# The left operands of a Strassen-type product: seven turned operands, or four turned blocks and sums of the turned blocks

## The chip, the cores and the metric

The kernel runs on 1 core of one Trainium2 chip. The metric is the time on the device in microseconds (us). The engines are TensorE (PE, matmuls; its weight loads are listed apart as PEld), VectorE (DVE), ScalarE (ACT), GpSimd (POOL) and SyncE (SP), which issues the DMAs of the part of the program that matters here.

## The reference

One encoder layer is computed for two requests with the same weights, x_prompt of 512 rows and x_sample of 1024 rows, all of width 1024, in fp32:

```python
h = _rmsnorm(x, norm_attn_g[l])
z = h @ w_in[l]
...
x = x + jnp.concatenate([a_out, c], axis=-1) @ w_out[l]
h = _rmsnorm(x, norm_ffn_g[l])
u = _dwconv(h @ w_up[l], ffn_dw_w[l], ffn_dw_b[l])
x = x + (jax.nn.silu(u[..., :D_FF]) * u[..., D_FF:]) @ w_down[l]
...
return _rmsnorm(x, norm_final_g)
```

a_out is windowed attention and c a convolution branch. D_FF is 2816. The change concerns `h @ w_up` of the sample: its left factor h, 1024 rows by 1024, is cut in four blocks of 512 by 512.

## The kernel before, in words

**The product.** The sample's up-projection is a product of the Strassen kind. For each of 22 column groups j there are seven block products of 512 x 512 (first to seventh in the code) in place of eight. Each is computed in a split precision: an operand is kept as hi and lo in fp32r, and each of four inner steps c takes three matmuls, whi by hi, whi by lo and wlo by hi (`prod`, L1080 to 1095; the matmuls are L1089 to 1091). The left operands are needed with the inner dimension on the partitions, so PE turns them: four transposes of 128 x 128 against an identity fill one PSUM bank (L1012), ACT copies the bank to hi (L1014) and DVE takes lo as bank minus hi (L965). A[i, c] holds the pair for operand i and step c. The operands 1 and 2 are the plain blocks of the sample's first 512 normalised rows, left and right half; the operands 3 to 7 are sums of blocks, or plain blocks of the last 512 rows.

**The stages.** The sample's rows come in eight blocks of 128, i = 4 to 11 in the code. `out_half` (L727) makes a row block of the output projection in matmuls L736 to 738, adds the residual (L741) and takes the sum of squares on ACT (L747); POOL makes the reciprocal root of it in two small operations (L186, L187); `scaled` (L978) multiplies the row block by it and by the norm's weights on DVE. For the last 512 rows `scaled` does this in two halves (L987) and then also takes the Strassen sums of the row blocks on DVE (s1, s2, the difference in place, and `last_sum`). `turned(1)` and `turned(2)` run in the out-projection stage, in banks called b. The other five, in the order 4, 6, 7, 5, 3, come after it in four banks called t: 80 transposes, put on PE between the matmuls of second(0), fourth(0) and second(1), seven, seven and eight groups of four (`every`, L1266 to 1276). Behind that come fourth(1), with two dummy matmuls (L1156) that open the accumulating bank for a copy from ACT (L1290), and sixth(0), sixth(1), seventh(0), seventh(1). A sixth product accumulates in a bank w; ACT copies the result out of the bank into a tile called u2 (L1172), and seventh accumulates in the same bank.

**What sets the order.** From `by_hand` (L1248) on PE's order is the order of the program; on the other engines, and on PE before, it is set by the scheduler when the program is built. Tiles in SBUF come from a list of slots (q, c, h, d and s, of fixed sizes and counts; h is the 128 x 512 one, 61 of them). A tile takes the slot that has been free the longest, and gives it back when the program drops its last name. An instruction that writes a reused slot waits until the readers of the tile that had it before are done. In the rows of the program below, h0_1252 is slot h0, tile number 1252. POOL takes the lo of the right operands (L965), from a hi that ACT makes (L1075).

Of the kernel before, what the change touches and what calls it, by code (L numbers as in the profile page):

```python
# [15 lines left out]
P = 128  # L16
# [132 lines left out]
def tile_hybrid_encoder(ctx: ExitStack, tc: tile.TileContext, xs, rel_bias, norm_attn_g, w_in,  # L149
# [811 lines left out]
    def add(out, a, b, eng=None):  # L961
        (eng or nc.vector).tensor_tensor(out, a, b, op=ALU.add)  # L962

    def sub(out, a, b, eng=None):
        (eng or nc.vector).tensor_tensor(out, a, b, op=ALU.subtract)  # L965
# [12 lines left out]
    def scaled(i):  # L978

        t, b = divmod(i - 4, 4)  # L980
        x = rows[t, b] = sb.tile([D])
        if t == 0:
            nc.vector.scalar_tensor_tensor(x[:], x1[i][:], rs2[:, i:i + 1], gFb[:], op0=ALU.mult, op1=ALU.mult)
            x1.pop(i)
            return
        for s in (R, L):
            nc.vector.scalar_tensor_tensor(x[:, s], x1[i][:, s], rs2[:, i:i + 1], gFb[:, s], op0=ALU.mult, op1=ALU.mult)  # L987
# [7 lines left out]
        if i >= NB - 2:  # L995
            last_sum(b)

    def last_sum(b):
        sub(rows[0, b][:, L], rows[0, b][:, R], rows["s2", b][:])

    def block_rows(i, b):
        if i in (1, 2, 3):
            return rows[0, b][:, R if i == 2 else L]
        if i in (4, 7):
            return rows[1, b][:, R if i == 4 else L]
        return rows["s1" if i == 5 else "s2", b][:]

    def turned(i, get):
        for c in range(4):
            held, ap = get()  # L1010
            for b in range(4):
                nc.tensor.transpose(ap[:, b * P:(b + 1) * P], block_rows(i, b)[:, c * P:(c + 1) * P], ident[:])  # L1012
            hi, lo = A[i, c] = (sb.tile([NT], F32R), sb.tile([NT], F32R))
            nc.scalar.copy(hi[:], ap)  # L1014
            sub(lo[:], ap, hi[:].bitcast(F32))
            held = None
            yield 0.0
        key = {6: "s2", 5: "s1", 7: 1, 3: 0}.get(i)
        for b in range(4):
            rows.pop((key, b), None)  # L1020

    def old_bank():
        b = bank("turn")
# [81 lines left out]
    for i in range(4, NB - 2):  # L1105
        if i + NE < NB:
            side.appendleft(conv_norm(i + NE))
        if i == 8:
            pace.update(rate=RE)
            side.appendleft(turned(1, old_bank))  # L1110
        for n in range(2):
            out_blocks(i, n)
    reserve(4)
# [1 line left out]
        for half in range(2):  # L1115
            load_up(j, half)
    drain(side)
    for b in range(2):
        last_sum(b)
# [6 lines left out]
    side.append(turned(2, old_bank))  # L1126
    sums_up(0)
    sums_up(1)
    out_blocks(NB - 2, 1)
# [35 lines left out]
    def second(j, between=None):  # L1165
        prod(st[j]["x"][:, L], j, 2, False, True, between)
# [7 lines left out]
    def fourth(j, between=None, start=False):  # L1174
        prod(st[j]["x"][:, R], j, 4, start, True, between)
# [79 lines left out]
    def chain(*gens):  # L1255
        for g in gens:
            yield from g
# [410 lines left out]
```

## Time and profile before

| | |
|---|---|
| median of three runs | 1549.37 us (1546.07 to 1552.7) |
| the profiled execution by itself | 1546.14 us |
| its span in the trace | 1544.4 us |
| mean granted clock of TensorE | 0.99 |
| TensorE busy | 1490.0 us, 96% of the span |
| ACT L1014, 128x512 hi from a t bank, in the stage | 590 ns |
| transposes L1012, into t / into b | 80 / 32 |

Times in the trace count from the start of the span. A row of the timeline gives the start, the duration, the engine, the line, the operation, output <- inputs by the program's names (slot numbers left out), the shape and how many like it run on; in brackets at its end stands how long its engine was idle before it, and what released it. A row of the waits gives the engine, the line and the releaser, then the total, the number of times and the longest. A row of the windows gives the stretch, its length, then busy us and number of instructions of PE, PEld, DVE, ACT and POOL, the granted clock, the share of time that the DMA engines were busy and GB/s.

### The profile page before, as it was taken

Reading aid. Unit: us, or ns where it says so; the run is one execution under the profiler, and the core shown is the slowest. Engines: PE = TensorE matmul, PEld = TensorE weight load, DVE = VectorE, ACT = ScalarE, POOL = GpSimd, SP = SyncE. Lnnn points to the kernel's source line nnn. Section 1 sums busy time; section 2 is a strip of 40 time slices with the busy share of each in tenths; the row PEclk is TensorE's granted clock in tenths of the full one; section 3 lists DMA queues with packets and bytes.
Section 4 is the critical chain, followed back from the end, with each engine's and each line's share of the span. In section 5 each row is a group of like instructions: output and inputs, shape, how many; then the busy total and the mean of one; then the engine's idle time right before and its main releaser. Section 6 shows DMA issues by size and latency. Waiting matters only on the chain. (4 is left out here: it accounts for less than half of the span.)

```text
span 1544.4 us, 20112 instructions
## 1 busy us (share of the span) xinstructions
PE 1490.0 (96%) x6843; PEld 1227.7 (79%) x6843; DVE 1126.2 (73%) x1604; ACT 795.5 (52%) x1404; POOL 710.7 (46%) x566
## 2 busy tenths in 40 slices
PE   8899998999999999899999999999999999999996
PEld 6787787787888888777777888888888788888885
DVE  6998767858789786344768777777776845569883
ACT  4644654335787786623454444545545543444354
POOL 7652343226666766957333555555554000003355
PEclk9999999899999999999999999999999999999998
DMA  6572334447344335769322233333331582357634
GB/s 229 160 214 79 108 98 129 130 135 226 112 130 134 117 124 182 245 234 300 129 80 87 86 102 108 112 106 105 103 116 67 194 291 83 106 167 235 220 136 164
DMA packets 228780, 227.17 MB, mean 147 GB/s; under 512 B 13268, under 2 KB 168348, under 8 KB 228549
## 3 DMA queue, kind: packets, MB, share of 16 engines
q1 hardware_dynamic: 228677, 225.88, 45.3%
q8 instruction: 54, 0.88, 0.2%
q14 instruction: 49, 0.40, 0.1%
HBM read 164.74 MB, written 62.14 MB: 147 GB/s over the span
## 5 line engine op out<-in xcount | busy, mean ns | idle before, releaser
L203 POOL TENSOR_TENSOR q<-q,q 128x1024 fp32r<-128x1024 f32 x72 | 173.5, 2415 | 91.5 <-ACT q L202 35.3
L965 POOL TENSOR_TENSOR q<-q,q 128x512 fp32r<-128x512 f32 x101 | 141.2, 1405 | 157.4 <-ACT q L1075 145.4
L965 DVE TENSOR_TENSOR h<-h,h 128x512 fp32r<-128x512 f32 (+2 forms) x202 | 153.8, 795 | 65.0 <-ACT h L969 24.4
L1423 PE MATMUL w<-h,h 128*128 128x512 f32 x462 | 179.8, 389 | 0.6 <-DVE q L1210 0.6
L1425 PE MATMUL w<-h,h 128*128 128x512 f32 x462 | 179.7, 389 | 0.0
L1424 PE MATMUL w<-h,h 128*128 128x512 f32 x462 | 179.7, 389 | 0.0
L1089 PE MATMUL w<-h,q 128*128 128x512 f32 x448 | 175.0, 391 | 2.9 <-ACT w L1181 1.2
L1091 PE MATMUL w<-h,q 128*128 128x512 f32 x448 | 174.4, 389 | 1.1 <-POOL q L965 1.1
L1090 PE MATMUL w<-h,q 128*128 128x512 f32 x426 | 165.8, 389 | 0.0
L309 PE MATMUL u<-h,q 128*128 128x512 f32 x400 | 159.4, 399 | 5.2 <-DVE h L862 4.3
L310 PE MATMUL u<-h,q 128*128 128x512 f32 x400 | 157.5, 394 | 0.0
L312 PE MATMUL u<-h,q 128*128 128x512 f32 x384 | 151.5, 394 | 2.8 <-POOL q L203 2.8
L962 POOL TENSOR_TENSOR q<-q,q 128x1024 f32<-128x1024 f32 x12 | 33.8, 2823 | 233.3 <-DMA h<-gb 194.4
L364 DVE SCALAR_TENSOR_TENSOR c<-c,cvw,c 128x512 f32<-128x512 f32 x184 | 138.0, 750 | 2.9
L969 ACT CAST h<-h 128x512 fp32r<-128x512 f32 x120 | 72.0, 620 | 93.2 <-DVE h L965 44.9
L309 PE MATMUL b<-h,q 128*128 128x512 f32 x256 | 102.3, 400 | 4.0 <-DVE d L394 3.0
L1423 PEld LDWEIGHTS w<-h,h 128*128 128x128 f32 x462 | 86.7, 188 | 19.1 <-ACT h L969 1.0
L862 DVE SCALAR_TENSOR_TENSOR h<-u,fw,h 128x511 f32<-128x511 f32 x88 | 65.5, 744 | 49.2 <-ACT h L866 48.4
L1089 PEld LDWEIGHTS w<-h,q 128*128 128x128 f32 x448 | 84.2, 188 | 21.4 <-ACT w L1181 1.6
L312 PE MATMUL b<-h,q 128*128 128x512 f32 x256 | 101.0, 395 | 0.0
L310 PE MATMUL b<-h,q 128*128 128x512 f32 x256 | 101.0, 394 | 0.0
L1425 PEld LDWEIGHTS w<-h,h 128*128 128x128 f32 x462 | 86.7, 188 | 18.0
(417 smaller groups left out, 3667.2 us busy)
## 6 DMA issues: line engine op xcount, KB each, us to landing
q<-in_w_up SPq DMA_DIRECT2D x88, 512.0 KB
ga<-q SPq DMA_DIRECT2D x64, 256.0 KB
h<-ga SPq DMA_DIRECT2D x57, 256.0 KB
q<-in_w_in SPq DMA_DIRECT2D x28, 512.0 KB
h<-in_w_down SPq DMA_DIRECT2D x52, 256.0 KB
q<-in_x_sample SPq DMA_DIRECT2D x15, 512.0 KB
h<-qsd SPq DMA_DIRECT2D x24, 256.0 KB
x1d<-q SPq DMA_DIRECT2D x11, 512.0 KB
```

The costliest lines, as they stand in the source:

```text
L203: (nc.vector if dve else nc.gpsimd).tensor_tensor(lo[:], raw[:], hi[:].bitcast(F32), op=ALU.subtract)
L309: nc.tensor.matmul(out, whi[:, kc, :], hi[:], start=(kc == 0), stop=False)
L310: nc.tensor.matmul(out, whi[:, kc, :], lo[:], start=False, stop=False)
L312: nc.tensor.matmul(out, wlo[:, kc, :], hi[:], start=False, stop=(kc == KC - 1))
L364: nc.vector.scalar_tensor_tensor(acc[:], src(t), w(t), acc[:], op0=ALU.mult, op1=ALU.add)
L965: (eng or nc.vector).tensor_tensor(out, a, b, op=ALU.subtract)
L1089: nc.tensor.matmul(out, whi[:, s], hi[:], start=(start and c == 0), stop=False, **go)
L1090: nc.tensor.matmul(out, whi[:, s], lo[:], start=False, stop=False, **go)
L1091: nc.tensor.matmul(out, wlo[:, s], hi[:], start=False, stop=(stop and c == 3), **go)
L1423: nc.tensor.matmul(out, sh[:, c], th[:], start=(p == 0), stop=False)
L1424: nc.tensor.matmul(out, sh[:, c], tl[:], start=False, stop=False)
L1425: nc.tensor.matmul(out, sl[:, c], th[:], start=False, stop=(p == NPAIR - 1))
```

## The change

`scaled` only scales, the whole row block of 1024 in one DVE operation (L982 of the changed kernel), and takes no sums. `turned_first` turns the two halves of the first 512 rows as before, and also copies each bank to a plain fp32 tile on ACT (L1002): eight copies more. `turned_rest` turns the two halves of the last 512 rows, in eight groups of four transposes (L989), 32 in place of 80: the left half's groups give operand 7's sum on DVE (plain minus bank), the right half's groups give operand 4 (hi on ACT, lo on DVE), the sum t on DVE, and the sum e on POOL (L962). All eight groups stand in second(0). `split_rest` then makes hi and lo of the operands 6, 7, 5 and 3 from the tiles in SBUF: hi on ACT (L993), lo on DVE, for operand 5 on POOL, and four differences f on DVE. fourth(0) and second(1) run without turns. Lines behind the diff are 22 to 24 higher in the changed kernel: the matmuls of `prod` are L1113 to 1115, the copy to u2 is L1194, the seed copy L1313, the dummy matmul L1178.

```diff
-        for s in (R, L):
-            nc.vector.scalar_tensor_tensor(x[:, s], x1[i][:, s], rs2[:, i:i + 1], gFb[:, s], op0=ALU.mult, op1=ALU.mult)
+        nc.vector.scalar_tensor_tensor(x[:], x1[i][:], rs2[:, i:i + 1], gFb[:], op0=ALU.mult, op1=ALU.mult)
         x1.pop(i)
-        e = rows[0, b]
-        s1 = rows["s1", b] = sb.tile([NT])
-        s2 = rows["s2", b] = sb.tile([NT])
-        add(s1[:], x[:, L], x[:, R])
-        sub(s2[:], s1[:], e[:, L])
-        sub(x[:, L], e[:, L], x[:, L])
...
+    def parts(i, c, src, eng=None):
+        hi, lo = A[i, c] = (sb.tile([NT], F32R), sb.tile([NT], F32R))
+        nc.scalar.copy(hi[:], src)
+        sub(lo[:], src, hi[:].bitcast(F32), eng)
+
+    def turned_first(i, get):
+        for c in range(4):
+            held, ap = get()
+            turn_in(0, (L, R)[i - 1], c, ap)
+            parts(i, c, ap)
+            p = plain[i, c] = sb.tile([NT])
+            nc.scalar.copy(p[:], ap)
...
+    def turned_rest(get):
+        s7 = []
+        for c in range(4):
+            held, ap = get()
+            turn_in(1, L, c, ap)
+            t = sb.tile([NT])
+            sub(t[:], plain[1, c][:], ap)
+            s7.append(t)
...
+        for c in range(4):
+            held, ap = get()
+            turn_in(1, R, c, ap)
+            parts(4, c, ap)
+            t, e, f = sb.tile([NT]), plain.pop((1, c)), plain.pop((2, c))
+            sub(t[:], ap, s7[c][:])
+            held = None
+            add(e[:], t[:], e[:], nc.gpsimd)
+            rest.append((c, t, s7[c], e, f))
...
+    def split_rest():
+        for n, i, eng in ((1, 6, None), (2, 7, None), (3, 5, nc.gpsimd), (4, 3, None)):
+            for k in range(4):
+                if i == 7:
+                    sub(rest[k][4][:], rest[k][4][:], rest[k][1][:])
+                    rest[k] = rest[k][:1] + (None,) + rest[k][2:]
+                parts(i, rest[k][0], rest[k][n][:], eng)
+                if i != 6:
+                    rest[k] = rest[k][:n] + (None,) + rest[k][n + 1:]
...
-    turns = chain(*(turned(i, turn_bank) for i in (4, 6, 7, 5, 3)))
+    turns = turned_rest(turn_bank)
...
-    second(0, every(7, turns))
-    fourth(0, every(7, turns), True)
-    second(1, chain(every(8, turns)))
+    second(0, every(8, turns))
     for _ in turns:
         raise RuntimeError("turns left")
+    split_rest()
+    fourth(0, None, True)
+    second(1)
```

The change moves instructions. On PE, at the end of the output projection, the program of before has these rows around the first group in a t bank (L738 is the last matmul of the output projection; w0 and w1 are the banks of first(0) and first(1); 16 more rows of first stand at the dots):

```order
L738 MATMUL c0_409_7740<-h3_1046_6618,h12_1205_7458 128x512
L1089 MATMUL w0_1_7882<-h6_1185_7373,q4_1222_7578 128x512
L1090 MATMUL w0_1_7882<-h46_1186_7374,q4_1222_7578 128x512
...
L1089 MATMUL w0_1_7882<-h17_1230_7674,q6_1223_7581 128x512 [waits Activation_49]
L1090 MATMUL w0_1_7882<-h5_1231_7675,q6_1223_7581 128x512
L1091 MATMUL w0_1_7882<-h17_1230_7674,q6_1223_7581 128x512
L1012 MATMUL t0_1_7915<-ident_91,q2_1200_7440 128x128 [waits DVE_49]
L1012 MATMUL t0_1_7915<-ident_91,q14_1219_7560 128x128
L1012 MATMUL t0_1_7915<-ident_91,c2_1238_7715 128x128
L1012 MATMUL t0_1_7915<-ident_91,q1_1253_7781 128x128 [waits DVE_49]
```

The changed program has these at the same place, all of them from the last L738 on:

```order
L738 MATMUL c0_409_7733<-h3_1046_6618,h15_1207_7460 128x512
L1115 MATMUL w1_2_7885<-h39_1187_7377,q7_1225_7606 128x512
L1113 MATMUL w1_2_7885<-h24_1190_7395,q7_1225_7606 128x512
L1114 MATMUL w1_2_7885<-h49_1191_7396,q7_1225_7606 128x512
L1115 MATMUL w1_2_7885<-h24_1190_7395,q7_1225_7606 128x512
L1113 MATMUL w0_1_7870<-h17_1230_7668,q6_1223_7575 128x512 [waits Activation_49]
L1114 MATMUL w0_1_7870<-h5_1231_7669,q6_1223_7575 128x512
L1115 MATMUL w0_1_7870<-h17_1230_7668,q6_1223_7575 128x512
L989 MATMUL t0_1_7903<-ident_91,q2_1204_7448 128x128 [waits DVE_49,Activation_49]
L989 MATMUL t0_1_7903<-ident_91,q14_1221_7562 128x128
L989 MATMUL t0_1_7903<-ident_91,c2_1241_7715 128x128
L989 MATMUL t0_1_7903<-ident_91,q1_1255_7776 128x128 [waits DVE_49]
```

Between the last matmul of the output projection and the transpose that reads the last scaled block (the one marked as waiting for DVE) stood 21 matmuls; now 7 do, and the other 14 stand ahead of that last matmul. The first transpose of the group has a wait for ACT too.

On ACT, from the two seed copies into the banks w2 and w3 on, the program of before has:

```order
L1290 COPY w2_3_8134<-h41_1256_7895 128x512 [waits PE_49]
L1290 COPY w3_4_8135<-h24_1257_7910 128x512 [waits PE_49]
L1172 COPY h28_1301_8168<-w2_3_8134 128x512 [waits PE_49,Pool_49]
L1172 COPY h26_1303_8185<-w3_4_8135 128x512 [waits PE_49]
L1185 COPY h41_1305_8214<-w2_3_8134 128x512 [waits PE_49,Activation_49]
```

The changed program has there, with the casts of split_rest (h20, h46, h13 and h42 are e of the four steps; h8, h14, h1 and h0 are f; L1194 copies the result of sixth to u2):

```order
L1313 COPY w3_4_8085<-h22_1257_7898 128x512 [waits PE_49]
L993 CAST h9_1290_8024<-h20_1183_7346 128x512 [waits DVE_49]
L993 CAST h20_1292_8028<-h46_1186_7363 128x512 [waits Pool_49]
L993 CAST h46_1294_8032<-h13_1189_7381 128x512 [waits Pool_49]
L1194 COPY h47_1309_8135<-w3_4_8085 128x512 [waits PE_49]
L993 CAST h13_1296_8036<-h42_1192_7399 128x512 [waits Pool_49]
L993 CAST h42_1297_8039<-h8_1232_7672 128x512 [waits Pool_49]
L993 CAST h8_1299_8043<-h14_1235_7689 128x512 [waits DVE_49]
L993 CAST h14_1300_8046<-h1_1240_7713 128x512 [waits DVE_49]
L993 CAST h1_1302_8050<-h0_1252_7749 128x512 [waits DVE_49]
L1194 COPY h0_1307_8118<-w2_3_8084 128x512 [waits DVE_49]
```

Where before the copy of u2 for the group j = 0 stood directly behind the seed copies, eight casts now stand between, and the copy writes slot h0, whose tile before is the last f. Each of these casts but the first writes the slot that the tile of the cast before it had: h20 is read by the first cast and written by the second, and so on. (In the rows that read these e, h20 is the tile numbered 1183, in the row behind it 1292.)

On DVE and POOL the lo operations between these casts stand in the changed program as follows, first four in a row on POOL (d, d and q are the slots of lo of operand 5), then four in a row on DVE (operand 3):

```order
L965 TENSOR_TENSOR d1_1291_8025<-h20_1183_7346,h9_1290_8024 128x512 [waits Activation_49]
L965 TENSOR_TENSOR d0_1293_8029<-h46_1186_7363,h20_1292_8028 128x512 [waits Activation_49]
L965 TENSOR_TENSOR q10_1295_8033<-h13_1189_7381,h46_1294_8032 128x512 [waits Activation_49]
L965 TENSOR_TENSOR q10_1295_8033<-h42_1192_7399,h13_1296_8036 128x512 [waits Activation_49]
L965 TENSOR_TENSOR q5_1298_8040<-h8_1232_7672,h42_1297_8039 128x512 [waits Activation_49]
L965 TENSOR_TENSOR q5_1298_8040<-h14_1235_7689,h8_1299_8043 128x512 [waits Activation_49]
L965 TENSOR_TENSOR q12_1301_8047<-h1_1240_7713,h14_1300_8046 128x512 [waits Activation_49]
L965 TENSOR_TENSOR q12_1301_8047<-h0_1252_7749,h1_1302_8050 128x512 [waits Activation_49]
```

The program of before has none of these eight; its lo of the same operands are taken from the banks t, and stand on DVE before the seed copies. seventh(0), the first matmul that waits for the copy of u2, reads h3_1282 and writes w2_3 in the changed program, and stands on PE right behind the 24 matmuls of sixth(0) and sixth(1).

More of the change, by code (lines that the diff above doesn't have):

```diff
@@ L1009, in turned, with turn_in @@
+        x1.pop(i)
+    plain = {}
+    def turn_in(t, s, c, ap):
+        for b in range(4):
+            nc.tensor.transpose(ap[:, b * P:(b + 1) * P], rows[t, b][:, s][:, c * P:(c + 1) * P], ident[:])
+    def parts(i, c, src, eng=None):
[3 more added lines that the diff above has]
+    def turned_first(i, get):
         for c in range(4):
             held, ap = get()
-            for b in range(4):
-                nc.tensor.transpose(ap[:, b * P:(b + 1) * P], block_rows(i, b)[:, c * P:(c + 1) * P], ident[:])
@@ L1013, in turned @@
-            hi, lo = A[i, c] = (sb.tile([NT], F32R), sb.tile([NT], F32R))
-            nc.scalar.copy(hi[:], ap)
-            sub(lo[:], ap, hi[:].bitcast(F32))
+            turn_in(0, (L, R)[i - 1], c, ap)
+            parts(i, c, ap)
+            p = plain[i, c] = sb.tile([NT])
+            nc.scalar.copy(p[:], ap)
             held = None
             yield 0.0
-        key = {6: "s2", 5: "s1", 7: 1, 3: 0}.get(i)
-        for b in range(4):
-            rows.pop((key, b), None)
+        if i == 2:
+            for b in range(4):
+                rows.pop((0, b))
@@ new lines, in turned_rest @@
+    def turned_rest(get):
[6 more added lines that the diff above has]
+            s7.append(t)
+            held = t = None
+            yield 0.0
+        for c in range(4):
[7 more added lines that the diff above has]
+            rest.append((c, t, s7[c], e, f))
+            s7[c] = t = e = f = None
+            yield 0.0
+        for b in range(4):
+            rows.pop((1, b))
@@ new lines, in tile_hybrid_encoder @@
+    rest = []
+    def split_rest():
[7 more added lines that the diff above has]
+                    rest[k] = rest[k][:n] + (None,) + rest[k][n + 1:]
+        rest.clear()
@@ L1117, in tile_hybrid_encoder @@
     drain(side)
-    for b in range(2):
-        last_sum(b)
     split_up(0, 1, 2)
```

19 lines of the change are left out of this document (2 added, 17 removed).

## The prediction

> **What bounds the kernel now.** I read the page's totals first, then PE's waits from 690 to 1200 us, the window that holds the change, and then the timeline of the turning stage.
>
> ```profile
> span 1544.4 us, 20112 instructions
> PE 1490.0 (96%) x6843; PEld 1227.7 (79%) x6843; DVE 1126.2 (73%) x1604; ACT 795.5 (52%) x1404; POOL 710.7 (46%) x566
> ```
> ```profile
> PE a L700 <- DMA h<-cvd: 1.3, 1, 1.3
> PE w L1091 <- POOL q L965: 1.1, 1, 1.1
> ```
> ```profile
> 782.00:812.00 30.00, 28.89 (x163) 23.10 (x162) 19.45 (x31) 18.15 (x34) 10.13 (x9) 1.00 0.25 80
> 820.00:1000.00 180.00, 178.88 (x789) 147.84 (x789) 144.95 (x139) 91.97 (x134) 94.11 (x66) 1.00 0.30 97
> ```
>
> PE is busy 96% of the span, and from 820 to 1000 us it lacks only 1.1 us of 180. So a PE instruction saved is time saved, and a PE wait added is time lost: at most that 1.1 us can be won back soon behind the stage. The turning stage is 782 to 812 us.
>
> **What it removes.** The price of a transpose comes from one step, three matmuls and eight transposes, on PE's timeline:
>
> ```profile
> 799.23 0.39 PE L1091 MATMUL w<-h,c 128*128 128x512 f32 x1
> 799.46 1.03 PE L1012 MATMUL t<-ident,h 128*128 128x128 f32 x8
> 800.80 0.39 PE L1091 MATMUL w<-h,c 128*128 128x512 f32 x1
> ...
> 813.94 0.39 PE L1090 MATMUL w<-h,h 128*128 128x512 f32 x1
> 814.16 0.39 PE L1091 MATMUL w<-h,h 128*128 128x512 f32 x1
> 814.39 0.39 PE L1089 MATMUL w<-h,q 128*128 128x512 f32 x1
> ```
>
> Matmuls start 0.227 us apart (813.94 to 814.39 is two steps), so of 1.57 us between the two L1091 three matmuls take 0.68, and each transpose 0.89 / 8 = 0.111 us. The change turns 32 instead of 80 transposes into the t banks: 48 x 0.111 = **5.3 us gained**. The window 782 to 812 holds 80 transposes and 83 matmuls, 8.9 + 18.8 = 27.7 us of 30: some **2.3 us** of stalls between the turns are lost there now, and go too, for the waits behind them are on groups that no longer exist.
>
> **What it puts in their place.** There are four places where PE waits anew. First, the cover of the last block's norm.
>
> ```profile
> 781.77 0.39 PE L738 MATMUL c<-h,h 128*128 128x512 f32 x1
> 782.69 0.68 DVE L741 TENSOR_TENSOR c<-c,c 128x512 f32<-128x512 f32 x1
> 784.04 1.06 ACT L747 ACTIVATE h<-c 128x1024 bf16<-128x1024 f32 x1
> 785.55 0.55 POOL L187 TENSOR_TENSOR rs<-rs,nhalf 128x1 f32<-128x1 f32 x1
> 786.14 1.41 DVE L987 SCALAR_TENSOR_TENSOR q<-c,rs,q 128x512 f32<-128x512 f32 x2 [2.17 <-POOL rs L187]
> 787.08 0.27 PE L1012 MATMUL t<-ident,q 128*128 128x128 f32 x1
> ```
>
> From the last out-block matmul at 781.77 to the transpose that needs the last normalised block, at 787.08, are 5.31 us. PE fills them exactly with 21 matmuls and three transposes (22 x 0.227 + 0.33 = 5.3). In the new order only 7 matmuls are left there, the other 14 stand ahead of the block, where PE was full anyway: 8 x 0.227 + 0.33 = 2.15. The chain itself stays (one L982 operation in place of two halves; DVE had two L965 in front of L741 that held it up by some 0.3 us). New wait: 2.6 to 3.2 us, I take **2.9**.
>
> Second, fourth(0), which used to run between turns, now follows them and wants the last hi and lo of operand 4.
>
> ```profile
> 789.22 0.68 DVE L965 TENSOR_TENSOR h<-t,h 128x512 fp32r<-128x512 f32 x1
> 792.22 0.67 DVE L965 TENSOR_TENSOR q<-q,h 128x512 f32<-128x512 f32 x1
> ```
>
> Each of the last four turn groups gives DVE two operations of 0.68 (lo, and the sum t), 1.36 us, against 4 transposes and 1.5 matmuls on PE, 0.78: four groups make 2.3 us. Two of the new f - t differences stand among them on DVE and can add 1.4. Bounds 2.3 and 3.7; I take **2.9**.
>
> Third, sixth(0) waits for the copy that seeds its bank (L1313), which is queued on ACT behind the last hi of operand 7; that waits for a tile that DVE and POOL must first let go.
>
> ```profile
> 787.46 1.29 POOL L965 TENSOR_TENSOR q<-h,q 128x512 fp32r<-128x512 f32 x1 [1.35 <-ACT q L1075]
> 787.59 1.71 DVE L962 TENSOR_TENSOR h<-q 128x512 f32<-128x512 f32 x1
> 792.31 1.74 POOL L965 TENSOR_TENSOR q<-h,q 128x512 fp32r<-128x512 f32 x1 [3.56 <-ACT q L1075]
> 792.82 4.46 DVE L965 TENSOR_TENSOR h<-t,h 128x512 fp32r<-128x512 f32 x7
> ```
>
> Nine DVE operations stand from the last t to lo 7: 6.1 us at 0.68, some 10.4 if half of them meet a POOL operation and take 1.71 as at 787.59; a cast and the copy add 1.2. Cover: 25 matmuls (the end of fourth(0), second(1), fourth(1)), 5.7 us. The wait is 1.6 to 5.9, or 0 if DVE runs ahead; I take **3.0**.
>
> Fourth, and largest: **the copy of u2 at the end of a serial chain**. Before, it stands right behind sixth(0):
>
> ```profile
> 811.92 0.59 ACT L1172 COPY h<-w 128x512 f32<-128x512 f32 x1 [2.22 <-PE w L1091]
> 814.59 0.59 ACT L1172 COPY h<-w 128x512 f32<-128x512 f32 x1 [2.08 <-PE w L1091]
> ```
> ```profile
> L1075 ACT CAST q<-h 128x512 fp32r<-128x512 f32 x11 | 6.8, 622 | 2.7 <-DMA ga<-q 2.1 <-DVE q L1227 0.6
> ```
>
> It empties w_3 before seventh(0) writes it, long before that is due (814.39). In the new order the copy (L1194) writes slot h0, the last tile of f, and comes after eight casts on ACT, each of which writes the tile that the lo before it has just read. The order is cast, lo on POOL, cast, lo on POOL, four times, then cast, lo on DVE, four times, then the copy. Eight casts at 0.62 are 5.0, four lo's on POOL at 1.29 are 5.2, four on DVE at 0.68 are 2.7, the copy 0.59: 13.5 us. Sixteen hand-overs at about 0.08 (from 791.61 + 0.62, the cast ahead of the POOL operation at 792.31) add 1.3. It begins some 0.6 us after sixth(0), behind the second seed copy: 15.4 us. PE has the 24 matmuls of sixth(0) and sixth(1) for it, 5.4 us. Wait: **10 us**, at least 8.5 if hand-overs cost nothing, 12 with POOL at 1.74. I take **9.5**, since part of the chain can start during the third wait.
>
> PE's clock falls after a long wait:
>
> ```profile
> 52.24 0.50 PE L309 MATMUL b<-h,q 128*128 128x512 f32 x1 [2.95 <-DVE d L394]
> ```
> ```profile
> 680.57 0.47 PE L736 MATMUL u<-h,h 128*128 128x512 f32 x1 [2.18 <-DVE s L703]
> 682.05 0.63 PE L736 MATMUL u<-h,h 128*128 128x512 f32 x1
> 682.48 0.63 PE L737 MATMUL u<-h,h 128*128 128x512 f32 x1
> ```
> ```profile
> 682.00:683.00 1.00, 1.00 (x4) 0.75 (x3) 0.74 (x1) 0.91 (x2) 1.00 (x3) 0.50 0.99 391
> 686.00:687.00 1.00, 1.00 (x6) 0.82 (x5) 0.67 (x1) 0.00 (x0) 1.00 (x3) 1.00 0.72 252
> ```
>
> After the 2.18 us wait at 680 the granted clock was 0.50 from 682 to past 685, and matmuls started 0.43 apart: eight of them lose 1.6 us. After a wait of 2.95 us at 52 it did not fall. For the 9.5 us I take one such dip, **1.6**; bounds 0 and 3.2 (a second dip for the shorter waits). The Trainium skill, page "TensorE: Matmul & The Clock Gate", Part 1, says that the array goes to half clock after an idle window of about 3.4 us and returns after as long a busy one. By that rule only the fourth wait would dip, an estimate of 1.7 us, and the sum would move by 0.1; the row at 680 shows that a shorter wait can do it too.
>
> The rest I cost at nothing: eight more plain copies on ACT (0.6 each, ACT is 52% busy); and the loads of cvd, which SP issues up to 13 rows later: the one wait for them is 1.3 us now, so plus or minus 1.
>
> **The sum.** -5.3 - 2.3 + 2.9 + 2.9 + 3.0 + 9.5 + 1.6 = +12.3 us. The profiled execution took 1546.1 us by itself (its span and 1.7 us around it), 3.2 below the median of the runs, 1549.4. So 1558.4 on its scale and 1561.7 on the median's; as some of the waits can run into each other I say **1561**. All low ends give -7.6 + 2.6 + 2.3 + 0 + 8.5 + 0 - 1.1 = +4.7, 1554; all high ends -7.6 + 3.2 + 3.7 + 5.9 + 12 + 3.2 = +20.4, 1570.
>
> **Rivals.** (a) *The chain is hidden, and the saving stays*: this decides if the casts of operands 5 and 3 get done before sixth(1) ends, that is, if the eight steps take under 5.4 us or start 10 us before sixth(0). For it speaks that ACT is only half busy; against it that each step waits for the step before. Time: -7.6 + 2.9 (the lost cover remains) = -4.7, so 1544.7; with that hidden too, 1541.8. (b) *DVE and POOL hinder each other all along*: POOL's 1.29 became 1.74 and DVE's 0.68 became 1.71 where they met; the new differences take both inputs from SBUF, while the seven at 792.82, which read a bank, ran at 0.64 beside POOL. The third wait is then 5.9 and the fourth 12: +17.7, 1567. The Trainium skill, "SBUF — State Buffer", section "SBUF: two separate sides", gives a rule for it: VectorE with two SBUF inputs and GpSimd reading SBUF exclude each other for a whole instruction. The two rows at 787 agree, 1.71 being about a wait for the end of 1.29 plus 0.68; by that rule the price is the same. (c) *Short waits*: the second and third waits vanish into each other, and the clock stays up: -7.6 + 2.6 + 2.3 + 8.5 = +5.8, 1555. (d) *The change does nothing measurable*, because PE's stalls only trade places: that would need the fourth wait at about half its least value, -7.6 + 2.6 + 1 + 4 = 0, 1549.
>
> **How the numbers follow.** The forecast has 0.5, (b) 0.18, (c) 0.15, (d) 0.07, (a) 0.10. Range 1549 to 1569: it takes in (b), (c) and (d), and leaves out (a) and a little beyond. A measurement of this kernel tells 0.5% from no change, 7.7 us: under 1541.7 is faster, over 1557.1 slower. (a) is mostly within the bound, 0.04 faster; (c), (d) and part of the forecast's lower flank are the same: 0.24; slower 0.72.
>
> **What would show it.** In the changed profile PE should wait once for about 9 us at the first L1113 of seventh(0), released by ACT L1194; PE should wait some 3 us at the fourth transpose of the first t group for DVE L982; the group L989 t should hold 32; on ACT the copies L1194 should follow eight casts L993 spaced 1.4 to 2.1 us apart; the granted clock should dip once behind the long wait. I am wrong if the chain of casts starts well before sixth(0), or if seventh(0) begins without a wait.

## The result, and the profile after

The changed kernel took **1567.49 us** (median of six runs, 1565.47 to 1570.11); the kernel before took 1547.74 us in its six (1544.38 to 1552.7). The ratio is **1.0125 [1.0105 to 1.0144]**: some 20 us slower. That is inside the range of 1549 to 1569, but above the 1561 that was forecast.

The page of the changed kernel, totals and the costliest group of matmuls:

```profile
span 1564.1 us, 20046 instructions
PE 1494.4 (96%) x6795; PEld 1228.7 (79%) x6795; DVE 1128.7 (72%) x1592; ACT 798.6 (51%) x1412; POOL 726.0 (46%) x574
L1113 PE MATMUL w<-h,q 128*128 128x512 f32 x416 | 165.3, 397 | 10.6 <-ACT h L1194 10.0
```

PE has 48 instructions fewer and is busy 4.4 us longer: some of them ran at a lower clock. The span grew by 19.7 us. PE's waits in the changed kernel, from 690 to 1200 us:

```profile
PE w L1113 <- ACT h L1194: 8.7, 1, 8.7
PE w L1113 <- ACT w L1313: 6.3, 1, 6.3
PE w L1114 <- DVE h L965: 2.8, 2, 2.0
PE a L700 <- DMA h<-cvd: 2.4, 2, 1.6
PE t L989 <- DVE q L982: 2.3, 1, 2.3
```

All four places of the forecast are there, each released by the line that was named. The row on cvd was 1.3 in the kernel before, and its 1.1 us of POOL are gone. PE's timeline in the changed kernel shows them in order, with the neighbours that are needed to measure them:

```profile
785.53 0.39 PE L738 MATMUL c<-h,h 128*128 128x512 f32 x1
...
787.57 0.27 PE L989 MATMUL t<-ident,c 128*128 128x128 f32 x1
790.12 0.59 PE L989 MATMUL t<-ident,q 128*128 128x128 f32 x3 [2.28 <-DVE q L982]
...
799.65 0.50 PE L1114 MATMUL w<-h,h 128*128 128x512 f32 x1 [0.79 <-DVE h L965]
...
802.57 0.50 PE L1114 MATMUL w<-h,h 128*128 128x512 f32 x1 [1.96 <-DVE h L965]
...
808.83 0.39 PE L1178 MATMUL w<-h 128*128 128x512 f32 x1
815.51 0.80 PE L1113 MATMUL w<-h,h 128*128 128x512 f32 x1 [6.30 <-ACT w L1313]
816.11 0.63 PE L1114 MATMUL w<-h,h 128*128 128x512 f32 x1
816.53 0.63 PE L1115 MATMUL w<-h,h 128*128 128x512 f32 x1
...
823.55 0.40 PE L1115 MATMUL w<-h,h 128*128 128x512 f32 x1
832.60 0.79 PE L1113 MATMUL w<-h,q 128*128 128x512 f32 x1 [8.65 <-ACT h L1194]
```

From start to start a wait costs some 0.15 us more than the bracket says: 808.83 to 815.51 is 6.68, less one matmul's 0.23 makes 6.45. After the wait the matmuls start 0.43 us apart (816.11, 816.53), not 0.227. The windows of the changed kernel behind three of the waits show the clock in the column before the last two:

```profile
790.00:793.00 3.00, 2.88 (x12) 2.49 (x13) 1.37 (x3) 1.76 (x3) 2.21 (x2) 0.58 0.34 103
817.00:820.00 3.00, 3.00 (x9) 2.35 (x8) 0.00 (x0) 0.69 (x2) 2.16 (x2) 0.50 0.00 0
835.00:838.00 3.00, 3.00 (x9) 2.32 (x8) 0.00 (x0) 0.00 (x0) 0.00 (x0) 0.50 0.00 0
862.00:1220.00 358.00, 357.56 (x1569) 293.45 (x1568) 279.10 (x258) 177.75 (x263) 191.81 (x131) 1.00 0.32 105
```

The last row says that behind the stage nothing is lost: nearly all of the 20 us lies between 780 and 862 us. The chain that the largest term rested on is on ACT's timeline of the changed kernel:

```profile
815.92 0.61 ACT L993 CAST h<-h 128x512 fp32r<-128x512 f32 x1
817.92 0.62 ACT L993 CAST h<-h 128x512 fp32r<-128x512 f32 x1 [1.39 <-POOL d L965]
...
823.98 0.59 ACT L1194 COPY h<-w 128x512 f32<-128x512 f32 x1 [3.44 <-PE w L1115]
...
827.83 0.62 ACT L993 CAST h<-h 128x512 fp32r<-128x512 f32 x1 [0.76 <-DVE q L965]
...
830.58 0.62 ACT L993 CAST h<-h 128x512 fp32r<-128x512 f32 x1 [0.76 <-DVE q L965]
831.96 0.59 ACT L1194 COPY h<-w 128x512 f32<-128x512 f32 x1 [0.76 <-DVE q L965]
```

Each bracket is the lo that still reads the tile which the next cast writes: a step takes 2.0 us with POOL and 1.37 us with DVE. From the first cast to the copy, at 831.96, are 16.0 us, and seventh(0) follows at 832.60. One step is longer than it had to be: the copy at 823.98 (u2 of j = 1) stands in the middle of the chain, waits there for the end of sixth(1), and holds up the fourth cast, which could have begun at about 822.5, by some 2 us.

### The profile page after: what moved, and what is told of

It reads as the page before. It is cut to its first block, busy times and chain, and to the rows that moved or that the text cites. A ratio compares the mean times of both kernels' runs of the same rounds, so it can differ in the third digit from the quotient of the medians.

```text
span 1564.1 us, 20046 instructions
## 1 busy us (share of the span) xinstructions
PE 1494.4 (96%) x6795; PEld 1228.7 (79%) x6795; DVE 1128.7 (72%) x1592; ACT 798.6 (51%) x1412; POOL 726.0 (46%) x574
## 5 line engine op out<-in xcount | busy, mean ns | idle before, releaser
L965 DVE TENSOR_TENSOR h<-h,h 128x512 fp32r<-128x512 f32 (+2 forms) x214 | 166.4, 810 | 67.0 <-DMA h<-in_w_down 23.6
L965 POOL TENSOR_TENSOR q<-q,q 128x512 fp32r<-128x512 f32 x82 | 113.7, 1399 | 155.3 <-ACT q L1099 149.7
L1113 PE MATMUL w<-h,q 128*128 128x512 f32 x416 | 165.3, 397 | 10.6 <-ACT h L1194 10.0
L1115 PE MATMUL w<-h,q 128*128 128x512 f32 x416 | 163.2, 392 | 0.0
L962 POOL TENSOR_TENSOR q<-q,q 128x1024 f32<-128x1024 f32 x12 | 33.4, 2792 | 232.8 <-DMA h<-gb 194.1
L1113 PEld LDWEIGHTS w<-h,q 128*128 128x128 f32 x416 | 79.0, 190 | 31.1 <-ACT h L1194 10.8
L1446 PEld LDWEIGHTS w<-h,h 128*128 128x128 f32 x462 | 86.7, 188 | 19.9 <-ACT h L969 1.9
L1448 PEld LDWEIGHTS w<-h,h 128*128 128x128 f32 x462 | 86.7, 188 | 18.1
L1447 PEld LDWEIGHTS w<-h,h 128*128 128x128 f32 x462 | 86.7, 188 | 17.8
```

The lines of the kernel that those rows point to most:

```text
L1113: nc.tensor.matmul(out, whi[:, s], hi[:], start=(start and c == 0), stop=False, **go)
L1115: nc.tensor.matmul(out, wlo[:, s], hi[:], start=False, stop=(stop and c == 3), **go)
L1446: nc.tensor.matmul(out, sh[:, c], th[:], start=(p == 0), stop=False)
L1447: nc.tensor.matmul(out, sh[:, c], tl[:], start=False, stop=False)
L1448: nc.tensor.matmul(out, sl[:, c], th[:], start=False, stop=(p == NPAIR - 1))
```

## The experiments

The theory that came out of this reading: the loss is the four new waits and the half clock behind them, and the third wait was longer than forecast because POOL's four additions ran beside DVE's differences. The rival: DVE, ACT and the slots have more to do behind the last turn than PE's matmuls there can hide, so that a wait that is taken away comes back at the next place. Each ratio is against the kernel before on the same chip. Where a kernel shifts the code, its line numbers differ by a few from the changed kernel's, and the text says so.

**1. u2slot: the copy of u2 for j = 0 gets another slot than h0.**

```diff
+        first_free = sb.tile([NT]) if j == 0 else None
         s["u2"] = sb.tile([NT])
+        first_free = None
```

> The changed kernel with one difference: the u2 tile of the group j = 0 gets another slot than h0, so that its copy does not stand behind the eight casts of operands 5 and 3. Theory (the copy at the end of the serial chain sets the fourth wait, 8.65 us at seventh(0), and the clock dip behind it costs some 2.6 us more): the wait for L1194 goes, the dip goes, 1567.5 - 11 = 1556. Rival 1 (the chain is needed anyway, for operands 5 and 3): the wait moves to fifth(0) or third(0) and the time falls by under 4, to 1564 or more. Rival 2 (something else releases seventh(0), as lo of operand 7): no change, 1567.

1562.67 us, ratio 1.0084 [1.0056 to 1.0112]. The wait at seventh(0) is gone, but PE's waits from 770 to 900 us in this kernel hold a new row:

```profile
PE w L1114 <- DVE q L965: 4.5, 3, 3.6
PE w L1113 <- ACT w L1315: 3.8, 1, 3.8
```

The 4.5 us are at third(0), the first product that reads operand 3, which begins 11 us behind the start of seventh(0): it waits for the lo's of operand 3, which stand on DVE between operations of the convolution in this kernel. So the slot was the cause of the fourth wait, and it hid a second one behind it. The 3.8 us are the third wait; it is shorter than 6.3 because PE is held up 2 us longer ahead of it: sixth(0) begins 29.6 us behind the last L738, against 30.0 in the changed kernel. Of some 20 us the kernel gives back about 6; the result lies between the theory and the first rival.

**2. noadd: without POOL's four additions.** Operand 5 is then a plain block.

```diff
-            add(e[:], t[:], e[:], nc.gpsimd)
```

> The changed kernel without the four additions on POOL that form operand 5 (it is left as a plain block, so the output is another). Theory (POOL and DVE hinder each other: seven DVE differences took 8.7 us instead of 4.8 while POOL worked from 803 to 809): POOL is done some 6 us earlier, DVE's differences take 0.7 to 0.9 each, the third wait falls from 6.3 to about 2.5, its clock dip mostly goes, and the time falls by 4 to 6, to 1562. Rival (the third wait is the serial hand-over between the casts of operand 7 and their lo, through reused slots): it falls by at most 1.5 and the time is 1566.

1560.49 us, ratio 1.0072 [1.0049 to 1.0096], by the ratios some 8 us less than the changed kernel. DVE's timeline of the changed kernel, and then POOL's, at the place of the third wait:

```profile
803.04 8.71 DVE L965 TENSOR_TENSOR h<-h,h 128x512 fp32r<-128x512 f32 x7
```
```profile
803.00 3.00 POOL L965 TENSOR_TENSOR q<-q,q 128x512 fp32r<-128x512 f32 x2
805.96 3.43 POOL L962 TENSOR_TENSOR h<-h,h 128x512 f32<-128x512 f32 x2
```

The same place on DVE's timeline without the additions, and PE's third and fourth wait there (its lines are one lower):

```profile
802.67 5.12 DVE L965 TENSOR_TENSOR h<-h,h 128x512 fp32r<-128x512 f32 x8
```
```profile
811.06 0.50 PE L1112 MATMUL w<-h,h 128*128 128x512 f32 x1 [0.56 <-ACT w L1312]
...
826.36 0.80 PE L1112 MATMUL w<-h,q 128*128 128x512 f32 x1 [9.56 <-ACT h L1193]
```

One DVE operation takes 8.71 / 7 = 1.24 us beside POOL and 5.12 / 8 = 0.64 without it, and the third wait falls from 6.30 to 0.56 us. The additions on POOL beside DVE are the cause of the third wait's size. (Two of the four stand beside the seven operations, with two lo's of right operands that the other two additions had delayed; in noadd POOL is done with those lo's at 802.67.) The fourth wait is 0.9 us longer: the chain from the first cast to the copy is 1.8 us shorter here (811.47 to 825.72), but the clock stays up behind the short third wait, and PE is through the 24 matmuls of sixth(0) and sixth(1) in 5.6 us instead of 8.3.

The page "SBUF — State Buffer" of the Trainium skill, section "SBUF: two separate sides", calls the port that VectorE and GpSimd share an exclusive lock for a whole instruction. The two rows agree in kind: 8.71 us less 7 x 0.64 leaves 4.2 us that DVE's operations took longer, beside 6.4 us in which POOL was busy.

**3. adddve: the same additions on DVE.**

```diff
-            add(e[:], t[:], e[:], nc.gpsimd)
+            add(e[:], t[:], e[:])
```

> The changed kernel with the four additions for operand 5 on DVE instead of POOL; nothing is left out. Theory (POOL and DVE hinder each other, a DVE difference takes 1.24 us instead of 0.69 beside POOL): four operations more on DVE cost 2.7 us, but the nine differences ahead of the third wait run nearer 0.8, which gives back 4 to 5: the third wait falls from 6.3 to about 4, the fourth stays near 9, the time is 1564. Rival (DVE's number of operations sets the third wait): it grows by 2.7 to 9, and the time is 1570.

1564.99 us, 1.0107 [1.0088 to 1.0126]. The third wait is 0.60 us here too, but the two waits inside fourth(0) grow from 2.8 to 5.0, since two of the additions stand on DVE ahead of the lo's that fourth(0) wants. Whether it is faster than the changed kernel at all the intervals do not say. The work on DVE before sixth(0), not only its neighbour, decides.

**4. swap: the turns in second(1) in place of second(0),** which puts 12 more matmuls ahead of the fourth transpose.

```diff
-    second(0, every(8, turns))
+    second(0)
+    second(1, every(8, turns))
...
-    second(1)
```

> The changed kernel with one exchange in PE's order: second(0) runs without turns, and the eight turn groups stand in second(1), so that 12 more matmuls stand ahead of the first turn group; fourth(0) follows the turns. Theory (the wait of 2.3 us at the fourth transpose comes from the lost cover of 14 matmuls): that wait goes, but the 12 matmuls are then missing behind the turns, where fourth(0) and sixth(0) wait for casts and differences that run on their own time, so their waits grow by as much: 1567 plus or minus 2. Rival (the wait at the fourth transpose is due to something else, such as DVE's queue ahead of L982): it stays, and the time is 1569 to 1570.

1566.29 us, 1.0112 [1.0093 to 1.0132]. PE's waits from 770 to 900 us in this kernel:

```profile
PE w L1113 <- ACT h L1194: 16.0, 1, 16.0
PE w L1114 <- DVE h L965: 3.4, 4, 2.7
```

The cover is back and the first wait gone; sixth(0) waits only 0.5 us. Apart from 2.9 us at fourth(0), all of it stands in one wait of 16.0 us at seventh(0), released by the same copy. Filling one gap moved the loss to the end of the chain and won nothing that can be measured.

**5. twice: the kernel before, with 48 of its transposes made twice.**

```diff
-                nc.tensor.transpose(ap[:, b * P:(b + 1) * P], ...)
+                for _ in range(2 if i in (6, 5, 3) else 1):
+                    nc.tensor.transpose(ap[:, b * P:(b + 1) * P], ...)
```

> The kernel of before with each of the 48 transposes of operands 6, 5 and 3 made twice into the same bank. Theory (a transpose in this stage costs PE its 0.111 us, since PE is full): 48 x 0.111 = 5.3 us, 1547.7 + 5.3 = 1553.0. Rival (the transposes fill gaps that the waits for ACT and DVE leave anyway): the 2.3 us of stalls between the turns shrink in return, +3 or less, 1550.7.

1551.44 us, 1.0014 [1.0002 to 1.0027], that is +2.2 us, between 0.3 and 4.2; in the trace the stage from the last L738 to seventh(0) grew by 3.1 us. 48 transposes at 0.111 are 5.3, so the rival was right. The difference is about the stalls between the turns: the 0.9 us wait for DVE's lo between them, for one, is not in this kernel's waits any more. So the two gains of the forecast are one: what the change can win at most on PE is transposes and stalls together, and while stalls are there a transpose costs less than its time.

**6. fill: 24 and 30 dummy matmuls ahead of sixth(0) and seventh(0),** to keep the clock up through the waits.

```diff
+    fill(24)
     sixth(0)
...
+    fill(30)
     seventh(0, None, False)
```

> The changed kernel with 24 dummy matmuls on PE ahead of sixth(0) and 30 ahead of seventh(0), into a bank that the next product clears; they wait for nothing and last 5.4 and 6.8 us, inside the waits of 6.3 and 8.65. Nothing is taken out. Theory (the half clock after the two waits costs about 12 matmuls times 0.2 us each time): the clock stays at 1.00, 24 matmuls run at 0.227 instead of 0.43 apart, 4.9 us saved, 1562.6. Rival (the dips are not due to idleness, or the saved time only lengthens the next wait, since the chains of casts run on their own time): the first dip's saving is eaten by the fourth wait, and 2.5 or 0 is saved, 1565 to 1567.5.

1576.85 us, 1.0186 [1.0156 to 1.0216]. The experiment failed. The dummies wrote the left half of the same tile w in whose right half sixth and seventh accumulate, and they waited for the copies into and out of that tile, as sixth and seventh do. PE's timeline in this kernel shows it:

```profile
813.29 8.19 PE L1178 MATMUL w<-h 128*128 128x512 f32 x24 [4.67 <-ACT w L1313]
830.84 8.73 PE L1178 MATMUL w<-h 128*128 128x512 f32 x30 [3.92 <-ACT h L1194]
```

They then added their own time to it, some of it at half clock. The run says nothing on what the clock costs.

**7. hand: DVE's order written out by hand,** with the turns in second(1), lo of operands 6 and 7 first on DVE, and the sums and casts of 5 and 3 behind sixth(1).

```diff
+    def split_53():
+        for k in range(4):
+            c, x, _, e, f = rest[k]
+            add(e[:], x[:], e[:], nc.gpsimd)
+            parts(5, c, e[:], nc.gpsimd)
...
+            sub(f[:], f[:], x[:])
+            parts(3, c, f[:])
...
-    by_hand = tc.manual_schedule(engines={mybir.EngineType.PE})
+    by_hand = tc.manual_schedule(engines={mybir.EngineType.PE, mybir.EngineType.DVE})
```

> The changed kernel with the turns in second(1), with lo of operands 6 and 7 ahead of everything for operands 5 and 3 in DVE's order, which is written out by hand here, and with the casts of operands 5 and 3 behind sixth(1); the four additions stay on POOL. Theory (the waits come from the order and from the slots, not from the amount of work): no wait at seventh(0) beyond 1 us, none at the fourth transpose; POOL still works beside DVE, so 2 to 5 us of waits stay at fourth(0) and sixth(0); the time is 1547 to 1552. Rival (DVE has too much to do in this stage: 20 operations are 14 us at 0.69): a wait of over 5 us stays and the time is over 1556.

1562.87 us, 1.0104 [1.0072 to 1.0136]: a miss. From the last L738 to seventh(0) it takes 27.1 us (the changed kernel 47.07, the kernel before 814.39 - 781.77 = 32.62), but PE waits 2.1 us at sixth(0), and for 1 to 3 us at several later products, for DVE among others.

**8. handd: as hand, with the additions on DVE.**

```diff
-            add(e[:], x[:], e[:], nc.gpsimd)
+            add(e[:], x[:], e[:])
```

> The kernel hand with the four additions on DVE, behind lo of operand 7, instead of on POOL early: the two differ in this alone. Theory (contention of DVE and POOL): all waits from the fourth transpose to seventh(0) are together under 3 us, the saving of the 48 transposes shows, 1542 to 1546, and 2 to 5 below hand. Rival (no contention; four more DVE operations): the same as hand or 1 to 3 above it, with a new wait at fifth(0).

1563.51 us, 1.0097 [1.0080 to 1.0115]: a miss again. The stage up to seventh(0) takes 22.6 us, which is 10.0 less than before; 3.2 of that are the 14 matmuls that stand ahead of it now, so 6.8 us are really won, about what the forecast took off (7.6). PE's waits in this kernel from 770 to 900 us (L1122 is the first matmul of a step):

```profile
PE w L1122 <- DVE q L1241: 6.1, 1, 6.1
PE w L1122 <- ACT h L1216: 2.6, 1, 2.6
```

And a window of this kernel further on, where the changed kernel's PE is busy throughout:

```profile
1000.00:1100.00 100.00, 95.93 (x410) 78.48 (x409) 62.61 (x67) 47.25 (x69) 50.17 (x35) 0.97 0.30 96
```

The gain is given back, and more, in two places above all: at a product that waits 6.1 us for DVE, which is late with the convolution behind sixth(1) (L1241), and by 2 to 4% in the loop (98.00 of the next 100 us), whose order on DVE the scheduler made anew. The clock falls behind both of the waits shown, too.

**9. hybrid: the kernel before, with only operands 5 and 3 made from the turned blocks,** 6 and 7 from row sums as before.

```diff
+            if i == 6:
+                add(plain[1, c][:], ap, plain[1, c][:])
+                sub(plain[2, c][:], plain[2, c][:], ap)
...
-    turns = chain(*(turned(i, turn_bank) for i in (4, 6, 7, 5, 3)))
+    turns = chain(*(turned(i, turn_bank) for i in (4, 7, 6)))
```

> The kernel of before with two operands turned less: the row-wise sums for operands 6 and 7 stay, ahead of the last block, and are turned; only operands 5 and 3 are taken from what is turned already, as plain block 1 plus the bank of operand 6 and plain block 2 minus it, by DVE straight from the bank (32 transposes less, eight plain copies more on ACT; turns of 4, 7 and 6 in second(0), fourth(0) and second(1)). Theory (what the change loses it loses because DVE's sums came to stand behind the last block, in SBUF beside POOL; here only eight sums do, out of a bank): 32 x 0.111 = 3.6 us gained and at most 2 lost, 1543 to 1547. Rival (the sums behind the last block cost as much however few they are): a wait of 3 us or more at sixth(0), fifth(0) or third(0), 1549 to 1553.

1581.05 us, 1.0211 [1.0192 to 1.0230]: a miss. The stage up to seventh(0) takes 30.6 us, 2.0 less than before; but six matmuls stand ahead of it here that stood in it before, which are 1.4 of the 2.0. Behind it PE has 92.6 to 94.1 us of each 100 in the loop from 900 to 1200, where before it had 99.6 to 100: again another order on DVE. The time therefore says little on the theory; the stage alone shows a gain of some 0.6 us, not of 3.6, since PE waits 2.6 us for ACT at the first dummy matmul of fourth(1).

**10. handx: handd without the eight sums of operands 5 and 3,** which are plain blocks then.

```diff
-            add(e[:], x[:], e[:])
...
-            sub(f[:], f[:], x[:])
```

> The kernel handd without the eight operations that form operands 5 and 3 on DVE (four additions, four differences; the operands are left as plain blocks, so the output is another). Theory (in handd DVE has no idle time from 823 to 844 and works off what the change put behind the last block, so the waits of 2.6, 6.1 and 1.4 us behind seventh(0) are its backlog): 5.5 us of DVE's work less take 5 to 8 us off, 1555 to 1558. Rival (these waits come from the order on ACT and the banks): under 2 us off, over 1561.

1554.33 us, 1.0035 [1.0023 to 1.0046]: 9 us less than handd for eight DVE operations of some 0.7 us, a little more than the 5 to 8 of the expectation. PE's two largest waits from 770 to 900 us in this kernel (L1239 is L1241's counterpart):

```profile
PE w L1120 <- ACT h L1201: 1.9, 1, 1.9
PE w L1120 <- DVE q L1239: 0.9, 1, 0.9
```

The loop from 900 to 1200 us is as short of work as handd's (94 to 99 of each 100 us), so the gain lies ahead of it: 5.2 us at L1241's counterpart, and the half clock that followed such waits in handd. DVE's backlog behind the last turn is thereby shown to be what holds PE up there in handd.

**11. handd5: handd with lo of operand 5 on DVE in place of POOL.**

```diff
-            parts(5, c, e[:], nc.gpsimd)
+            parts(5, c, e[:], None)
```

> The kernel handd with lo of operand 5 on DVE instead of POOL, nothing left out. Theory (beside the four operations of POOL from 808.8 to 815.4 DVE's run at 1.2 to 1.8 us instead of 0.69): DVE gets four more operations, 2.8 us, and gains about as much from the absent contention; 1563 plus or minus 2. Rival (contention is the larger part): 1558 or less. Rival (DVE's count is the larger part): 1567 or more.

1561.41 us, 1.0085 [1.0066 to 1.0104]. Four more operations on DVE and none of POOL beside it: the two cancel within the intervals, as was expected, and the wait stands at ACT's copy instead (6.4 us).

**12. mend3: DVE's order by hand again,** with the additions on DVE, the sums and casts of 5 and 3 ahead of fourth(0) in the program, and u2 in another slot. In the loop DVE has nearly the changed kernel's order. The lines are against handd.

```diff
+            add(e[:], x[:], e[:])
+            sub(f[:], f[:], x[:])
...
+        first_free = sb.tile([NT]) if j == 0 else None
         s["u2"] = sb.tile([NT])
+        first_free = None
...
-    split_67()
+    split_rest()
...
-    split_53()
```

> The kernel handd with the casts, lo and sums of operands 5 and 3 emitted ahead of fourth(0) again, and u2 of the group 0 in another slot than h0; DVE's order in the turning stage is the same as in handd (lo of 6 and 7, then the eight sums, then lo of 3), lo of 5 on POOL. What differs is DVE's order in the steady loop from 860 to 1220 us, which the scheduler makes: here it is the same as in the changed kernel, where PE had 357.6 of 358 us, while in handd it is another one, with 94 to 98 of 100. Theory (handd gained 7 us up to seventh(0), lost some 13 behind it to DVE's backlog, and another 10 to that order): the loop is full again and the time is 8 to 11 below handd's ratio, 1552 to 1556. Rival (the loop is short because of the backlog, not the order): PE in the loop stays at 94 to 98 of 100 and the time is 1560 or more.

1559.98 us, 1.0072 [1.0046 to 1.0099]. First a window of the loop in this kernel, then PE's largest wait from 770 to 900 us (L1119 is the first matmul of a step):

```profile
1000.00:1100.00 100.00, 100.00 (x440) 82.25 (x440) 81.39 (x76) 50.95 (x74) 54.14 (x37) 1.00 0.33 108
```
```profile
PE w L1119 <- DVE q L1240: 7.1, 1, 7.1
```

The loop is full again although the backlog is still there, so its loss in hand and handd went with the order. By the ratios this is some 4 us less than handd, within the intervals, and not the 8 to 11 of the expectation: the stage up to seventh(0) takes 24.1 us, and what it wins is lost to 7.1 us of waiting for DVE, to some 5 us of short waits and to the half clock behind them. None of the twelve beats the kernel before. Of those with operands made from the turned blocks that still compute everything, the best, this one, u2slot and handd5, remain 0.7 to 0.9% slower.

## Why the prediction was right, and where it was too small

The terms can be read from the profiled executions, the first two only together (-7.2; the table splits them by the price of a transpose). The stage from the last L738 to seventh(0) went from 32.62 to 47.07 us. The 14 matmuls that moved ahead of it, 3.2 us, are in no row, since they cost as much there; what else lies ahead of it and behind it is in the row before the sum.

| step | forecast | measured |
|---|---|---|
| 48 transposes less | -5.3 | -5.3 (the group L989 t holds 32; 48 x 0.111, a price and not a measurement) |
| old stalls between the turns | -2.3 | about -1.9 (what is left over of the stage's sum) |
| fourth transpose | +2.9 | +2.4 (787.57 to 790.12, less 0.11) |
| fourth(0) | +2.9 | +3.1 (0.95 and 2.13) |
| sixth(0) | **+3.0** | **+6.5** (808.83 to 815.51, less 0.23) |
| seventh(0) | +9.5 | +8.8 (823.55 to 832.60, less 0.23) |
| the clock | **+1.6** | **+6.7** (1.5 + 2.6 + 2.6) |
| ahead of the stage; behind it | 0 | +0.6 (cvd +1.1, a wait in the b banks -0.5); -1.1 (POOL's wait) |
| sum | +12.3 | +19.8 (the spans differ by 19.7) |

The direction, the four places, their order, the releasing lines and the steps of the chain through the reused slots were **right**. That the chain cannot be hidden (rival a) was right too, and that the waits could run into one another (rival c) did not come true: all four stand side by side. That 9.5 was said for seventh(0) and 8.8 came out is partly luck. The chain did not start during the third wait, as "I take 9.5" had it, but 0.4 us behind the start of sixth(0). It was 1.7 us longer than the 15.4 of the working, because the copy of j = 1 stands behind the third cast and not behind the eighth. And PE had 8.3 us to cover it instead of 5.4, because sixth(0) ran at half clock. In noadd, where the clock stays up there and the copy of j = 1 holds up nothing by more than 0.8 us, the stretch from sixth(0) to seventh(0) is 15.3 us, as in the working, and the wait is 9.6.

Two terms were **too small**, by 3.5 and 5.1 us; the miss is 7.5, since the others came out 1.1 lower. The first is the step "I take 3.0" for sixth(0). The working had the right two prices for a DVE operation, 0.68 alone and 1.71 beside POOL, but took a value near the middle; in the run seven operations in a row met POOL and took 1.24 each on average. The run noadd shows that the additions make the wait: without them it is 0.56 us. The wait is also a little above the bound of 5.9. ACT's timeline of the changed kernel shows why:

```profile
812.68 0.62 ACT L993 CAST h<-h 128x512 fp32r<-128x512 f32 x1 [0.31 <-DVE h L965]
814.36 0.62 ACT L993 CAST h<-h 128x512 fp32r<-128x512 f32 x1 [1.05 <-DVE h L965]
814.88 1.10 ACT L1313 COPY w<-h 128x512 f32<-128x512 f32 x2
```

The last casts of operand 7 wait for a DVE operation each, by the chain's pattern the lo that still reads the slot they write; these hand-overs were counted for the fourth wait and not for the third. This is rival (b)'s mechanism at one of its two places; at the other, seventh(0), POOL ran at 1.27 us apart from one operation, and the wait stayed under 9.5. The 1567 that (b) gave is nearly the result, but its sum reached it with a longer fourth wait and with one dip of the clock.

The second is the step "I take one such dip, 1.6". There were three, and each of the two behind the long waits slowed 12 matmuls in place of 8: from 815.51 to 820.80 they took 5.29 us, where 12 x 0.227 are 2.72, so 2.6 are lost. The first came after the wait of 2.28 us, where matmuls and transposes that take 2.12 us at full clock took 3.66 from 790.12 to 793.78. The row at 680 us had shown that 2.18 us can be enough; it was used as a bound and should have been a term, though not a sure one, as the last section shows. The Trainium skill, page "TensorE: Matmul & The Clock Gate", Part 1, gives an idle window of about 3.4 us for the fall and as much sustained work for the return. Here the trace differs from it on the fall: the clock fell behind 2.28 us of waiting. The return took some 5.3 us of work after each of the two long waits (815.51 to 820.80, and 832.60 to 837.88), longer than one such window.

The deeper cause is not one of the four places, and the experiments that repair them one by one show it. Before the change the Strassen sums were taken of rows, on DVE, while later row blocks were still on their way; behind the last scaled block 24 DVE operations were left (four sums of that block, and 20 lo's straight from the banks). In the changed kernel 28 operations on DVE and 8 on POOL stand behind it. Sums of turned blocks can begin only behind the turn of the last block. So the sums, the casts of operands in SBUF and their hand-overs all stand behind that point, in a stretch in which PE has some 65 matmuls, 15 us, to hide them under. Take the slot away (u2slot), the cover's gap (swap) or POOL (adddve), and the loss stands at the next place; take eight operations from DVE (handx), and 9 us go. What the change saves on PE is real, 6.8 us in handd's stage, but it is smaller than what it moves. That the backlog is the one cause of all four places is argued from these runs; it is shown only for the waits of handd that handx removes.

Two things stay open. What the half clock costs by itself was not measured apart, since fill failed; the 6.7 us are read off the distances between starts. And whether an order exists that keeps the saving, with the loop full and DVE in time, was not settled: mend3 came nearest, and its remaining 11 us are named by their releasers but were not tested one by one.

## What to carry to other kernels

When a change moves work from before the last input's arrival to behind it, count that work on every engine against what the busiest engine can still hide there; the instructions saved on the busiest engine are the smaller number. If a repair of one wait moves the time by less than the wait, look for the same producer at the next consumer, and test the producer's load (as handx does), not the next wait. Price the half clock as likely, not as sure, behind a wait of two us or more (here 2.1 to 2.7 us brought it in most kernels, and 2.95 us at 52 did not), and a tile that is written in the slot its predecessor has just left as a chain, step by step.

## What the hardware showed that was not expected

- **The same wait can drop the clock or not.** The wait for L982 is 2.28 us in the changed kernel, in u2slot, in adddve, in fill and in noadd. The three us that follow it have a granted clock of 0.58, 0.60 and 0.53 in the first three, and 1.00 in the other two; in these it falls later, behind the short waits of fourth(0) (to 0.67 in noadd, 0.52 in fill), where the changed kernel's does not fall. Here are noadd's windows there; the changed kernel has 1.00 in both:

```profile
802.00:805.00 3.00, 2.80 (x9) 2.27 (x10) 3.00 (x6) 0.62 (x1) 0.68 (x1) 0.76 0.78 213
805.00:808.00 3.00, 3.00 (x10) 2.33 (x10) 2.65 (x5) 1.29 (x3) 0.00 (x0) 0.67 0.49 142
```

- **The scheduler's order in a distant loop** (no fact of the chip) cost up to as much as the change itself: PE had 92.6 to 98.7 us of 100 in the loops of hand, handd, handx, handd5 and hybrid, and all 100 in mend3's. In hybrid that is 19 us of 300.
